# Sums of the seven products' weights made in DRAM, and the other half of the tokens normalized first

## The chip, the cores and the metric

The kernel runs on one core of a Trainium2 chip. TensorE (PE) multiplies matrices, its weights loaded by a unit of its own (PEld); VectorE (DVE) and ScalarE (ACT) work on whole tiles; GpSimd (POOL) does little here but issue transfers; SyncE (SP) issues the others. All transfers run on the core's 16 DMA engines, POOL's through the queue that the profile calls software_dynamic, SP's through hardware_dynamic. The metric is the device time of one execution in microseconds.

## What is computed

Two layers of a hybrid block over 512 latent tokens and 256 context tokens with 1024 channels. Each layer normalizes, runs three mixers side by side (convolution, attention, retention), merges them through gates and an output projection, and then a gated feed-forward part. For layer 0 it runs on all 768 tokens, and it is what the change is about:

```python
def conv_ffn(h, w_up, dw_w, dw_b, w_down):
    gt, val = jnp.split(h @ w_up, 2, axis=-1)
    gt = dwconv(gt, dw_w, dw_b)
    return (jax.nn.silu(gt) * val) @ w_down
...
        y = merge_branches(gates, a, att, ret, w_pa[l], w_pb[l], w_pc[l]) @ w_out[l]
        x = x + g1 * y
...
        x = x + g2 * conv_ffn(modulate(rms_norm(x, norm2_g[l]), sh2, sc2),
                              w_up[l], ffn_dw_w[l], ffn_dw_b[l], w_down[l])
        if not last:
            xc = xc + cg2 * conv_ffn(modulate(rms_norm(xc, norm2_g[l]), csh2, csc2),
                                     w_up[l], ffn_dw_w[l], ffn_dw_b[l], w_down[l])
```

`modulate` uses one shift and scale for the latent tokens and others for the context.

## The kernel before

Activations stand with channels in partitions and tokens along the row, in tiles of 128 channels x 768 tokens, latent tokens (0 to 511) ahead of the context (512 to 767). A product in fp32 is made of three matmuls: weight and token operand are each split into a high and a low part (hi is ACT's copy in a rounded format, lo is DVE's difference), and hi x hi, hi x lo and lo x hi are added up in PSUM.

**Weights.** A stream of tiles (class `Stream`) of 128x1024 fp32, 512 KB each, is loaded by SP from `wstream` into buffers `raw`. `prepare` splits them some tiles ahead of use: ACT at L224 (whi), DVE at L225 (wlo), into a rotating set of slots that come free when PE has used the tile in them.

**Seven products.** `up_seven` in `ffn` makes w_up's product for layer 0, in 22 chunks of 128 columns. Weights and tokens are cut in two by two blocks (channels 0 to 511 and 512 to 1023; gate and value columns; first and second half of the tokens, 384 each), and seven products take the place of eight. Of the weights these need the blocks 11, 12 and 22 as they are and S1 = 21 + 22, S2 = 11 + S1, S3 = 11 + 21, S4 = 12 + S2. `operand` makes the four sums per chunk with four additions on DVE (L188) in the raw tiles, and ACT and DVE split each operand by itself (tiles wop, 128x512). Of the tokens, `split_tokens` makes the operands in two goes: after tokens 0 to 383 are normalized, those of 11 and 12; after tokens 384 to 767, those of S2, S1, S3, 22 and S4, in that order. A go normalizes blocks b (DVE L691, ACT L693) of 384 tokens; the second half crosses token 512, so its blocks are made in pieces of 128 and 256. t2 and t3 are the sums (L716, L717, L722, L730), hh and hl their split parts. PE goes through the products in `up_order`: 11 and 12 of chunks 0 to 2, then S2 of all three (`s2_first`, both halves of its four channel blocks in turn), S1, S3, and so on. `product` (L1693) is the line of all their matmuls.

**Before that stage**, `last_chunks` makes w_out's last four output chunks half by half (`parts`), so that the first half of the tokens can be normalized while the second is multiplied.

**Mixers.** Layer 0 runs the steps of the string `ORDER[0]` one after the other ('K Q0 R0 Q1 A R1 G0 C G1 G2 G3 P0 ...'): dense products of the step, with attention and retention run beside them in pieces. On POOL's queue in that stage stand `attsp<-att` (an attention result, 384 KB, written to DRAM from a tile in a shared set of slots, four times), `ij<-ij` (a table that retention's decay factors kdec and dec are made of) and, from 470 us, rowa.

**Residual updates.** After every four chunks a down phase multiplies by w_down; its results dx are added to xup in DRAM by accumulating transfers (POOL, `accum_op`), 32 in all.

A scheduler orders each engine's instructions; within an engine they run in that order, and a transfer is issued by its engine in its turn, after what it waits for.

Of the kernel before, what the change touches and what calls it, by code (L numbers as in the profile page):

```python
# [25 lines left out]
P = 128  # L26
# [23 lines left out]
ATTR, RETR, CONVR, ADAR = (1.0, 1.0), (1.4, 1.6), (0.4, 0.4), (0.06, 0.28, 0.4, 0.33)  # L50
QLAG = 2
# [64 lines left out]
def up_blocks(c, row, half):  # L116

    return [(("w_up", 0, (4 * half + j) * P, row * DFF + c * P), P) for j in range(4)]
# [10 lines left out]
class Stream:  # L129
# [3 lines left out]
    def __init__(self, k, dram):  # L133
        self.k, self.dram = k, dram


        self.items, self.units, self.need, self.blocks = [], [0], [], []
        self.ab, self.de = {}, {}

        def load():  # L140
            self.blocks.append([])
            return len(self.blocks) - 1

        def tiles(n):
            for _ in range(n):
                self.items.append(load())
                self.units.append(self.units[-1] + 2)
                self.need.append(len(self.blocks))
        tiles(NUP)
        for x in up_order():  # L150
# [16 lines left out]
        self.raw, self.s1 = {}, {}  # L167
# [6 lines left out]
        self.tag = 0  # L174

    def issue(self, upto):
        while self.issued < min(upto, self.need[self.limit - 1]):
            i = self.issued
            t = self.k.raw_pool.tile([P, SUB], F32, tag="raw", name=f"raw{i}")
            self.k.nc.sync.dma_start(t, self.dram[i])  # L180
            self.raw[i] = t
            self.issued += 1

    def operand(self, name, c):

        nc = self.k.nc
# [12 lines left out]
        if name == "S2":  # L199
            self.s1[c] = self.k.S("s1")[:, :Q]  # L200
            add(self.s1[c], d, e)
            add(e, a, e)
            add(a, self.s1[c], a)
            return a
        return self.s1.pop(c) if name == "S1" else e

    def prepare(self, base):
# [3 lines left out]
        while self.done < self.limit and self.units[self.done + 1] - self.units[base] <= 2 * WB:  # L211
# [42 lines left out]
    def next_operand(self, *x):  # L254
        self.step()
        self.off = SUB
        assert self.items[self.cur] == x
        return self.split[self.cur]
# [29 lines left out]
class Kern:  # L288
# [32 lines left out]
    def mm(self, out, w, x, start, stop):  # L321
        return self.nc.tensor.matmul(out, w, x, start=start, stop=stop)  # L322
# [58 lines left out]
    def last_chunks(self, key, xs, segs, hold, evac, norm, lead=0, limit=None):  # L381
# [23 lines left out]
        halves = parts(segs)  # L405
# [211 lines left out]

    def rstd2(self, pts, name, y=None):
# [55 lines left out]
    def split_tokens(self, l, xs, ops):  # L674
# [19 lines left out]

        def parts(name, t, i):
            ops.setdefault(name, [None, None])[i] = self.split(t, TALL, "h")

        def gen(segs):
# [3 lines left out]
            if not half:  # L702
# [783 lines left out]
    def run(self):  # L1486
        nc, io = self.nc, self.io
        self.ada_blocks = []
        self.sq2 = self.crow = None
        self.setup()  # L1490
# [35 lines left out]
    def layer_mixers(self, l, last, segs, T, xs, xsp, first, h2):  # L1526
# [38 lines left out]
        for step in ORDER[l].split():  # L1565
# [48 lines left out]
        def evac(m, pts):  # L1614
            for pt, o, c in kinds(pts):
# [7 lines left out]
                                None if l else NUP + 2 * UPFIRST)  # L1623

    def ffn(self, l, h2, xs, segs, T, gen, xsp, xup):
# [57 lines left out]
        def up_seven():  # L1683
# [12 lines left out]
            one, two = slice(0, HALF), slice(HALF, TALL)  # L1696
# [260 lines left out]
```

## Time and profile before

| | |
|---|---|
| time, median of 3 runs | 2299.3 us (2297.7 to 2299.55) |
| profiled execution, its own time | 2294.79 us |
| its span | 2293.0 us |
| PE busy | 2226.6 us, 97% |
| DVE busy | 1665.9 us, 73% |
| ACT busy | 998.2 us, 44% |
| POOL busy | 104.3 us, 5% |
| DMA, mean | 106 GB/s; q1 (SP) 169.03 MB, q0 (POOL) 72.36 MB |

The profile is of one execution. Busy time is an engine's own; the lists of waits name the engine that waited, its tile and line, and after the arrow what released it. Times of single instructions are from the start of the span. The seven-product stage runs from about 815 to 1290 us, layer 0's mixers from about 100 to 600.

### The profile page before, as it was taken

The numbers are of one execution on the slowest core, as the hardware profiler recorded it, in microseconds if no ns is written. First come the engines' busy times: TensorE is split into PE (matmuls) and PEld (weight loads), VectorE is DVE, ScalarE is ACT, GpSimd is POOL, SyncE is SP. The second block draws the span as 40 slices with busy tenths as digits, with TensorE's granted clock in tenths as the row PEclk, the third lists the DMA queues.
The fourth block names the chain that finished last, engine by engine and source line by source line (L and its number), as shares of the span: only waits on it lengthen the run. The fifth ranks groups of instructions, "written<-read, shape, count | busy, mean of one in ns | idle before, by whom it ended". The sixth has DMA issues, their size and how long they took to land.

```text
span 2293.0 us, 34300 instructions
## 1 busy us (share of the span) xinstructions
PE 2226.6 (97%) x13386; PEld 2033.7 (89%) x13386; DVE 1665.9 (73%) x3384; ACT 998.2 (44%) x1784; POOL 104.3 (5%) x177
## 2 busy tenths in 40 slices
PE   6999999999999979999999999999999999999998
PEld 4988999999999969999999889888887889888887
DVE  6877959799885488676676769878799656744445
ACT  3465653332332256455454444665443334423333
POOL 0000000000010000100101100000001100000000
PEclk9999999999999989999999999999999999999999
DMA  8211111123343202544635412111126623422221
GB/s 316 100 68 54 45 56 46 38 92 138 121 165 120 77 36 109 138 113 118 156 96 144 182 74 75 51 51 61 56 87 236 236 93 106 170 101 94 100 92 37
DMA packets 70961, 243.57 MB, mean 106 GB/s; under 512 B 8496, under 2 KB 10816, under 8 KB 70800
## 3 DMA queue, kind: packets, MB, share of 16 engines
q1 hardware_dynamic: 50400, 169.03, 20.9%
q0 software_dynamic: 20400, 72.36, 11.0%
q8 instruction: 105, 1.72, 0.3%
q14 instruction: 56, 0.46, 0.1%
HBM read 218.82 MB, written 22.54 MB: 105 GB/s over the span
## 4 chain that ended last, share of the span: by engine, by line
PE 85%; DVE 6%; issue 5%; ACT 2%; DMA 2%; POOL 0%; SPq 0%; DVEq 0%; POOLq 0%; ACTq 0%
PE pd L322 57%; PE ps L322 14%; PE pd L1693 10%; PE ps L1693 2%; PE ps L1350 2%; DVE wlo L225 1%; PE ps L1263 0%; ACT whi L224 0%; DMA x<-xt 0%; DMA rowa<-wadt 0%; DMA xup<-dx 0%; DVE cacc L799 0%; DMA raw<-wstream 0%; DVE fy L1742 0%; DVE qq L1298 0%
## 5 line engine op out<-in xcount | busy, mean ns | idle before, releaser
L224 ACT ACTIVATE whi<-raw 128x1024 fp32r<-128x1024 f32 x236 | 249.7, 1060 | 637.2 <-PE pd L322 496.0
L322 PE MATMUL pd<-hh,whi 128*128 128x384 f32 (+2 forms) x1472 | 470.5, 359 | 0.0
L322 PE MATMUL pd<-hh,wlo 128*128 128x384 f32 (+2 forms) x1472 | 470.4, 359 | 0.0
L322 PE MATMUL pd<-hl,whi 128*128 128x384 f32 (+2 forms) x1472 | 469.7, 359 | 0.0
L225 DVE TENSOR_TENSOR wlo<-raw,whi 128x1024 fp32r<-128x1024 f32 x236 | 288.1, 1222 | 180.3 <-ACT whi L224 176.5
L322 PEld LDWEIGHTS pd<-hh,whi 128*128 128x128 f32 x1472 | 270.6, 188 | 28.2 <-issue 1.7
L322 PEld LDWEIGHTS pd<-hh,wlo 128*128 128x128 f32 x1472 | 271.5, 188 | 25.8 <-issue 1.1
L322 PEld LDWEIGHTS pd<-hl,whi 128*128 128x128 f32 x1472 | 270.9, 188 | 25.6 <-issue 0.7
L1693 PE MATMUL pd<-hh,wop 128*128 128x384 f32 x1024 | 267.5, 337 | 18.9 <-ACT wop L224 16.4
L799 DVE SCALAR_TENSOR_TENSOR cacc<-u,vec,cacc 128x497 f32<-128x497 f32 (+9 forms) x360 | 221.0, 650 | 2.0
L1693 PEld LDWEIGHTS pd<-hh,wop 128*128 128x128 f32 x1024 | 186.6, 189 | 21.3 <-ACT wop L224 16.7
L1693 PE MATMUL pd<-hl,wop 128*128 128x384 f32 x512 | 172.3, 337 | 0.0
L1333 ACT ACTIVATE prob<-ps,amx,qrs 128x256 f32<-128x256 f32 (+1 forms) x144 | 93.8, 656 | 90.4 <-DVE amx L1328 75.2
L322 PE MATMUL pd<-whi,hl 128*128 128x256 f32 x416 | 118.9, 287 | 5.5 <-DVE hl L756 5.5
L322 PE MATMUL pd<-whi,hh 128*128 128x256 f32 x416 | 119.3, 289 | 1.7 <-ACT hh L753 1.7
L322 PE MATMUL pd<-wlo,hh 128*128 128x256 f32 x416 | 117.9, 284 | 0.0
L224 ACT ACTIVATE wop<-raw 128x512 fp32r<-128x512 f32 x132 | 81.1, 627 | 65.4 <-DVE raw L188 24.5
L322 PE MATMUL pd<-hidh,whi 128*128 128x512 f32 (+1 forms) x302 | 104.4, 358 | 2.8 <-DVE x L1783 2.8
L225 DVE TENSOR_TENSOR wop<-raw,wop 128x512 fp32r<-128x512 f32 x132 | 87.7, 687 | 25.0 <-ACT wop L224 24.4
L322 PE MATMUL pd<-hidl,whi 128*128 128x512 f32 (+1 forms) x302 | 103.5, 355 | 0.0
L322 PE MATMUL pd<-hidh,wlo 128*128 128x512 f32 (+1 forms) x302 | 103.3, 355 | 0.0
L601 DVE SCALAR_TENSOR_TENSOR rowa<-rowa,crow 128x768 f32<-128x768 f32 (+1 forms) x144 | 94.4, 686 | 4.0 <-DMA rowa<-wadt 4.0
(299 smaller groups left out, 4279.5 us busy)
## 6 DMA issues: line engine op xcount, KB each, us to landing
raw<-wstream SPq DMA_DIRECT2D x280, 512.0 KB, 3.5
rowa<-wadt POOLq DMA_DIRECT2D x72, 512.0 KB, 4.5
xup<-dx POOLq DMA_DIRECT2D x32, 384.0 KB, 5.9
adar<-wada SPq DMA_DIRECT2D x16, 384.0 KB, 7.6
rawa<-wada SPq DMA_DIRECT2D x8, 512.0 KB, 4.2
x<-xt SPq DMA_DIRECT2D x8, 384.0 KB, 7.7
crow<-crow POOLq DMA_DIRECT2D x8, 384.0 KB, 4.3
x<-xt POOLq DMA_DIRECT2D x8, 384.0 KB, 4.4
```

Source lines behind the costliest of these rows:

```text
L224: nc.scalar.activation(hi, r, AF.Copy)
L225: nc.vector.tensor_tensor(lo, r, hi.bitcast(F32), op=ALU.subtract)
L322: return self.nc.tensor.matmul(out, w, x, start=start, stop=stop)
L601: nc.vector.scalar_tensor_tensor(out, raw[:, a:b], 1.0, t[:, o:o + b - a], op0=ALU.mult, op1=ALU.mult, accum_out=acc[:, c, j, h:h + 1])
L799: nc.vector.scalar_tensor_tensor(acc[:, a:b], u[:, a + d:b + d], w(k), acc[:, a:b], op0=ALU.mult, op1=ALU.add)
L1333: nc.scalar.activation(pr[:, o - k0:o - k0 + c], pt[:, :c], AF.Exp, scale=rs, bias=mx[:, 2:3], accum_out=sm[:, j:j + 1])
L1350: nc.tensor.transpose(pt[:, b * P:b * P + P], pr[:, o + b * P:o + b * P + P], self.ident)
L1693: nc.tensor.matmul(pt, w[:, b], x, start=start and k == 0 and i == 0, stop=k == 3 and i == 2, skip_group_check=not start)
```

## The change

The weights of the blocks 11, 12, 21 and 22 come as inputs of their own (`wup0` to `wup23`), for six batches of four chunks, the last of two; they are no longer in `wstream`. `make_sums` is called after the steps named in `SUMAT` and makes S1, S3, S2 and S4 of a batch in DRAM: a copy of one block, then a transfer that adds another to it (S2 adds S1, S4 adds S2), all issued by POOL. The first copies of a batch wait for the last matmul that was written down before the call. In `Stream` the operands go in pairs: a raw tile is filled by two loads of 256 KB, from the blocks or from the sums, and split whole, 128x1024, at one line with the other weights; `operand` and its DVE additions are gone. `last_chunks` takes the halves in the other order where the seven products follow, `split_tokens` makes 11 and 12 of tokens 384 to 767 and the rest after tokens 0 to 383, and `one` and `two` change places with that. Of the second go, all sums and splits that are not S2's are ordered behind S2's last split on DVE.

```diff
@@ -48,6 +48,7 @@
          'K Q0 Q1 R0 A G0 C R1 G1 G2 G3 P0 P1 P2 P3 T T T T T T')
 ATT_LEAD, RET_LEAD = (3, 2), (1, 1)
 ATTR, RETR, CONVR, ADAR = (1.0, 1.0), (1.4, 1.6), (0.4, 0.4), (0.06, 0.28, 0.4, 0.33)
+SUMAT = ("R1", "G1", "G2", "G3", "P1", "P2")
 QLAG = 2
 HOLDO, HOLDD = (4, 4), (4, 6)
 LEADO, LEADD, LEADB = 2, 2, ((0, 0, 0), (4, 0, 4))
@@ -113,9 +114,26 @@
...
-def up_blocks(c, row, half):
-    return [(("w_up", 0, (4 * half + j) * P, row * DFF + c * P), P) for j in range(4)]
+BATCH = 4
+BLOCKS = ("11", "12", "21", "22")
+SUMS = (("S1", "21", ("22",)), ("S3", "11", ("21",)), ("S2", "11", ("S1",)), ("S4", "12", ("S2",)))
+def batches():
+    return [range(c, min(c + BATCH, NFF)) for c in range(0, NFF, BATCH)]
@@ -152,57 +171,38 @@
...
-            name, c = x
-            if name == "11":
-                self.ab[c] = load()
-                self.blocks[-1] = up_blocks(c, 0, 0) + up_blocks(c, 0, 1)
-            elif name == "S2":
-                self.de[c] = load()
-                self.blocks[-1] = up_blocks(c, 1, 1) + up_blocks(c, 1, 0)
-            self.items.append(x)
-            self.units.append(self.units[-1] + 1)
-            self.need.append(len(self.blocks))
-        tiles(DEPTH * NSUB - len(self.blocks))
+            if n % 2 == 0:
+                tiles(1)
+                self.blocks[-1] = None
+                self.ops[self.items[-1]] = []
+            self.ops[self.items[-1]].append(x)
+            self.place[x] = (len(self.items) - 1, Q * (n % 2))
+            n += 1
+        tiles(DEPTH * NSUB - 8 * NFF // 4 - sum(x is not None for x in self.blocks))
...
-            self.k.nc.sync.dma_start(t, self.dram[i])
+            if i in self.ops:
+                for j, x in enumerate(self.ops[i]):
+                    self.k.nc.sync.dma_start(t[:, j * Q:j * Q + Q], self.k.up_operand(*x))
+            else:
+                self.k.nc.sync.dma_start(t, self.dram[self.row(i)])
...
-    def operand(self, name, c):
-        nc = self.k.nc
-        a, b = (self.raw[self.ab[c]][:, o:o + Q] for o in (0, Q))
-        add = lambda out, x, y: nc.vector.tensor_tensor(out, x, y, op=ALU.add)
-        if name == "11":
-            return a
-        if name == "12":
-            return b
-        if name == "S4":
-            add(b, a, b)
-            return b
-        d, e = (self.raw[self.de[c]][:, o:o + Q] for o in (0, Q))
-        if name == "22":
-            return d
-        if name == "S2":
-            self.s1[c] = self.k.S("s1")[:, :Q]
-            add(self.s1[c], d, e)
-            add(e, a, e)
-            add(a, self.s1[c], a)
-            return a
-        return self.s1.pop(c) if name == "S1" else e
@@ -212,15 +212,9 @@
             i = self.done
             x = self.items[i]
             self.issue(self.need[i])
-            if isinstance(x, tuple):
-                r = self.operand(*x)
-                t = pool.tile([P, SUB], F32R, tag=("whi", "wlo")[self.tag], name=f"wop{i}")
-                self.tag = 1 - self.tag
-                hi, lo = t[:, :Q], t[:, Q:]
-            else:
-                r = self.raw.pop(x)
-                hi = pool.tile([P, SUB], F32R, tag="whi", name=f"whi{i}")
-                lo = pool.tile([P, SUB], F32R, tag="wlo", name=f"wlo{i}")
+            r = self.raw.pop(x)
+            hi = pool.tile([P, SUB], F32R, tag="whi", name=f"whi{i}")
+            lo = pool.tile([P, SUB], F32R, tag="wlo", name=f"wlo{i}")
             nc.scalar.activation(hi, r, AF.Copy)
             nc.vector.tensor_tensor(lo, r, hi.bitcast(F32), op=ALU.subtract)
             self.split[i] = (hi, lo)
@@ -319,7 +316,8 @@
         return self.small.tile([P, cols], F32, tag=tag, name=self.nm(tag))
     def mm(self, out, w, x, start, stop):
-        return self.nc.tensor.matmul(out, w, x, start=start, stop=stop)
+        self.last_mm = self.nc.tensor.matmul(out, w, x, start=start, stop=stop)
+        return self.last_mm
     @contextmanager
@@ -402,7 +400,7 @@
                     tiles.append(self.W.cur)
         tiles.append(self.W.cur + (self.W.off == SUB))
         gen = None
-        halves = parts(segs)
+        halves = parts(segs)[::-1] if limit else parts(segs)
         for i, hs in enumerate(halves):
             for j, m in enumerate(range(KC - hold, KC)):
                 evac(m, self.dense(None, xs, hs, ws[j]))
@@ -615,6 +613,25 @@
...
+    def up_operand(self, name, c):
+        b, j = divmod(c, BATCH)
+        t = self.up_sums[b][name] if name in self.up_sums[b] else self.io[f"wup{4 * b + BLOCKS.index(name)}"]
+        return t[:, j * Q:j * Q + Q]
+    def make_sums(self, b):
+        n = len(batches()[b]) * Q
+        src = {x: self.io[f"wup{4 * b + i}"] for i, x in enumerate(BLOCKS)}
+        for name, base, more in SUMS:
+            t = src[name] = self.up_sums[b][name] = self.dram.tile([P, n], F32, name=f"sum{name}_{b}")
+            first = self.nc.gpsimd.dma_start(t, src[base], max_dma_last_dim=2048)
+            info = mybir.DependencyInfo(mybir.DependencyClass.Sync, mybir.DependencyReason.DATA)
+            self.tc.add_manual_dep(first.ins, self.last_mm.ins.name, info, reason="later")
+            for x in more:
+                self.nc.gpsimd.dma_start(t, src[x], accum_op=ALU.add, max_dma_last_dim=2048)
@@ -692,14 +709,25 @@
...
+        done = []
         def parts(name, t, i):
-            ops.setdefault(name, [None, None])[i] = self.split(t, TALL, "h")
+            hi, lo = ops.setdefault(name, [None, None])[i] = self.S("hh", F32R), self.S("hl", F32R)
+            nc.scalar.activation(hi, t, AF.Copy)
+            op = nc.vector.tensor_tensor(lo, t, hi.bitcast(F32), op=ALU.subtract)
+            (done.append if name == "S2" else later)(op)
+        def later(op):
+            if done:
+                info = mybir.DependencyInfo(mybir.DependencyClass.NoSync, mybir.DependencyReason.DATA)
+                self.tc.add_manual_dep(op.ins, done[-1].ins.name, info, reason="order")
         def gen(segs):
             half = segs[0][0]
             self.sq_rstd(segs, r)
             yield
-            if not half:
+            if half:
@@ -719,7 +747,7 @@
             yield "S2"
             for i in range(2):
                 u, b = raw["u", i], raw["11", i]
-                nc.vector.tensor_tensor(u, b, u, op=ALU.subtract)
+                later(nc.vector.tensor_tensor(u, b, u, op=ALU.subtract))
                 parts("S1", u, i)
             yield "S1"
             for i in range(2):
@@ -727,7 +755,7 @@
             yield "S3"
             for i in range(2):
                 b = raw["12", i]
-                nc.vector.scalar_tensor_tensor(t2[i], t2[i], -1.0, b, op0=ALU.mult, op1=ALU.subtract)
+                later(nc.vector.scalar_tensor_tensor(t2[i], t2[i], -1.0, b, op0=ALU.mult, op1=ALU.subtract))
                 parts("22", t2[i], i)
             yield "22"
             for i in range(2):
@@ -1582,6 +1611,8 @@
                 self.ret_in[i] = self.ret_inputs(i, segs, T)
             elif kind == "T":
                 ths.append(self.gate(2, len(ths), segs))
+            if l == 0 and step in SUMAT:
+                self.make_sums(SUMAT.index(step))
         self.finish(mix)
         if l == 0:
             self.finish(ada)
@@ -1620,7 +1651,7 @@
         norm = self.norm(l, 1, xs, h2) if last else self.split_tokens(l, xs, h2)
         return self.last_chunks(lambda m, k: ("w_out", l, k * P, m * P), mm, even(segs), HOLDO[l], evac, norm, LEADO,
-                                None if l else NUP + 2 * UPFIRST)
+                                None if l else NUP + UPFIRST)
     def ffn(self, l, h2, xs, segs, T, gen, xsp, xup):
         nc = self.nc
@@ -1693,7 +1724,7 @@
                         nc.tensor.matmul(pt, w[:, b], x, start=start and k == 0 and i == 0, stop=k == 3 and i == 2,
                                          skip_group_check=not start)
-            one, two = slice(0, HALF), slice(HALF, TALL)
+            one, two = slice(HALF, TALL), slice(0, HALF)
             def p11(c):
                 X[c], g[c], val[c] = self.dps()[:, :HALF], self.S("fg"), self.S("fv")
```

On POOL, in the mixers' stretch around the third and fourth attention step, there stood before:

```order
L1469 DMA attsp1_103<-att_375_2472 128x768
L1469 DMA attsp2_104<-att_483_3043 128x768
L1554 DMA ij_646_3940<-ij 128x514
L1469 DMA attsp3_105<-att_590_3664 128x768
L590 DMA rowa0_2_0_5548<-wadt 128x1024
```

and now, from the last sum of batch 2 on (the sums' names end in the batch, counted from 0; L627 are plain copies, L632 accumulating ones):

```order
L632 DMA sumS4_2_3101<-sumS2_2_3098 512x512
L632 DMA sumS1_3_3433<-wup15 512x512
L627 DMA sumS3_3_3436<-wup12 512x512
L627 DMA sumS2_3_3439<-wup12 512x512
L632 DMA sumS3_3_3436<-wup14 512x512
L632 DMA sumS2_3_3439<-sumS1_3_3433 512x512
L627 DMA sumS4_3_3442<-wup13 512x512
L1497 DMA attsp2_104<-att_483_3067 128x768
L632 DMA sumS4_3_3442<-sumS2_3_3439 512x512
L1583 DMA ij_646_3988<-ij 128x514
L1497 DMA attsp3_105<-att_590_3712 128x768
```

The transfers attsp2, ij and attsp3, which stood one behind the other, now stand behind and between those of batches 2 and 3.

On ACT, in the last attention step before retention, there stood (prob and probt are the attention weights, kdec retention's factors; the semaphores that each waits for are in brackets):

```order
L1333 ACTIVATE prob_636_3886,asm_635_3883<-ps_633_3879,amx_634_3882,qrs_118_830 128x256 [waits DVE_49,Activation_49]
L1351 ACTIVATE probt_637_3890<-ps_638_3891 128x256 [waits PE_49]
L1365 ACTIVATE att_590_3664<-ps_639_3895 128x128 [waits PE_49]
L1351 ACTIVATE probt_640_3917<-ps_641_3918 128x256 [waits PE_49]
L1351 ACTIVATE probt_642_3922<-ps_643_3923 128x256 [waits PE_49]
```

and now:

```order
L1361 ACTIVATE prob_636_3934,asm_635_3931<-ps_633_3927,amx_634_3930,qrs_118_830 128x256 [waits DVE_49,Activation_49]
L1379 ACTIVATE probt_637_3938<-ps_638_3939 128x256 [waits DMASW5_49,PE_49]
L1393 ACTIVATE att_590_3712<-ps_639_3943 128x128 [waits PE_49]
L1379 ACTIVATE probt_640_3965<-ps_641_3966 128x256 [waits PE_49]
L1379 ACTIVATE probt_642_3970<-ps_643_3971 128x256 [waits PE_49]
```

The order is the same; probt_637 now has the slot of the tile that attsp2 reads, and waits for that transfer's landing (DMASW5).

On DVE, at the start of the seven-product stage, from the last pieces of the second go on, there stood:

```order
L691 SCALAR_TENSOR_TENSOR b_1103_8429<-x_963_6899,coef0_86,rstd_1039_7736 128x256
L730 SCALAR_TENSOR_TENSOR t2_1099_8413<-t2_1099_8413,b_1072_8205 128x768
L716 TENSOR_TENSOR t3_1104_8438<-b_1103_8429,b_1102_8420 128x768
L717 SCALAR_TENSOR_TENSOR t2_1105_8439<-t3_1104_8438,b_1069_8196 128x768
L722 TENSOR_TENSOR b_1102_8420<-b_1069_8196,b_1102_8420 128x768
L451 TENSOR_TENSOR hl_1107_8443<-t2_1105_8439,hh_1106_8442 128x768
L188 TENSOR_TENSOR s1_1108_8448<-raw77_8446 128x512
L188 TENSOR_TENSOR s1_1109_8459<-raw78_8455 128x512
L188 TENSOR_TENSOR raw77_8446<-raw74_7928,raw77_8446 128x512
L188 TENSOR_TENSOR raw78_8455<-raw75_7988,raw78_8455 128x512
```

and now, from the pair splits that stand among the second go's first part on:

```order
L219 TENSOR_TENSOR wlo79_8536<-raw79_8525,whi79_8535 128x1024
L744 TENSOR_TENSOR t3_1098_8489<-b_1097_8484,b_1096_8479 128x768
L219 TENSOR_TENSOR wlo80_8543<-raw80_8532,whi80_8542 128x1024
L745 SCALAR_TENSOR_TENSOR t2_1099_8490<-t3_1098_8489,b_1064_8227 128x768
L717 TENSOR_TENSOR hl_1101_8494<-t2_1099_8490,hh_1100_8493 128x768
L708 SCALAR_TENSOR_TENSOR b_1102_8497<-x_958_6961,coef0_86,rstd_1039_7808 128x384
L708 SCALAR_TENSOR_TENSOR b_1102_8497<-x_959_6963,coef0_86,rstd_1039_7808 128x384
L708 SCALAR_TENSOR_TENSOR b_1103_8502<-x_962_6969,coef0_86,rstd_1039_7808 128x384
L708 SCALAR_TENSOR_TENSOR b_1103_8502<-x_963_6971,coef0_86,rstd_1039_7808 128x384
L744 TENSOR_TENSOR t3_1104_8507<-b_1103_8502,b_1102_8497 128x768
L745 SCALAR_TENSOR_TENSOR t2_1105_8508<-t3_1104_8507,b_1069_8273 128x768
L717 TENSOR_TENSOR hl_1107_8512<-t2_1105_8508,hh_1106_8511 128x768
```

The blocks are made in one piece, the additions of L188 are gone, L722 and L730 (now L750 and L758) follow behind hl_1107, and the pair splits wlo78 to wlo80 stand ahead of S2's first split.

## Rows read from the trace of the kernel before

**Rows 1.** Head of the page: busy us (share of the span) xinstructions.

```profile
PE 2226.6 (97%) x13386; PEld 2033.7 (89%) x13386; DVE 1665.9 (73%) x3384; ACT 998.2 (44%) x1784; POOL 104.3 (5%) x177
```

**Rows 2.** Waits of PE: line <- released by: us in total, times, longest us.

```profile
PE pd L1693 <- ACT wop L224: 16.4, 1, 16.4
...
PE ps L322 <- ACT dx L1774: 2.7, 5, 1.1
```

**Rows 3.** Timeline of PE, 820 to 870: start us, us, instruction [idle before <-releaser].

```profile
828.16 0.34 PE L1693 MATMUL ps<-hh,wop 128*128 128x384 f32 x1
844.90 0.69 PE L1693 MATMUL pd<-hh,wop 128*128 128x384 f32 x1 [16.41 <-ACT wop L224]
```

**Rows 4.** Timeline of DVE, 817 to 845.

```profile
817.54 1.14 DVE L691 SCALAR_TENSOR_TENSOR b<-x,coef,rstd 128x384 f32<-128x384 f32 x2
...
833.86 2.72 DVE L691 SCALAR_TENSOR_TENSOR b<-x,coef,rstd 128x128 f32<-128x128 f32 x8
...
840.22 0.96 DVE L451 TENSOR_TENSOR hl<-t,hh 128x768 fp32r<-128x768 f32 x1
841.10 1.28 DVE L188 TENSOR_TENSOR s<-raw 128x512 f32<-128x512 f32 x2
```

**Rows 5.** Windows: us, busy us (xinstructions) of PE, PEld, DVE, ACT, POOL, PEclk, DMA share, GB/s.

```profile
845.00:851.00 6.00, 5.87 (x18) 5.36 (x19) 6.00 (x11) 4.33 (x8) 0.00 (x0) 0.51 0.00 0
851.00:861.00 10.00, 10.00 (x59) 10.00 (x58) 8.77 (x13) 6.59 (x12) 0.00 (x0) 1.00 0.30 100
...
1000.00:1050.00 50.00, 50.00 (x290) 50.00 (x289) 34.25 (x67) 24.82 (x47) 9.09 (x12) 1.00 0.69 166
...
300.00:350.00 50.00, 49.81 (x399) 45.52 (x396) 29.74 (x70) 21.18 (x56) 1.08 (x2) 1.00 0.13 46
```

**Rows 6.** Page, costliest groups: xcount | busy, mean ns | idle before.

```profile
L225 DVE TENSOR_TENSOR wlo<-raw,whi 128x1024 fp32r<-128x1024 f32 x236 | 288.1, 1222 | 180.3 <-ACT whi L224 176.5
```

**Rows 7.** Timeline of POOL, 190 to 400 and 1000 to 1060.

```profile
292.51 0.54 POOL L1469 DMA_DIRECT2D attsp<-att  x1 [42.25 <-ACT att L1365]
318.06 0.54 POOL L1554 DMA_DIRECT2D ij<-ij  x1 [25.00 <-DVE u L773]
...
1017.91 0.85 POOL L1775 DMA_DIRECT2D xup<-dx  x1 [10.07 <-ACT dx L1774]
```

**Rows 8.** Timeline of ACT, 208 to 226 and 318 to 336.

```profile
212.09 0.78 ACT L1333 ACTIVATE prob<-ps,amx,qrs 128x512 f32<-128x512 f32 x1 [1.61 <-issue]
...
322.26 0.39 ACT L1351 ACTIVATE probt<-ps 128x256 f32<-128x256 f32 x1
...
325.18 0.48 ACT L888 ACTIVATE kdec<-lg,ij 128x8 f32<-128x8 f32 x2
```

**Rows 9.** Timeline of PE, 318 to 336.

```profile
333.25 1.16 PE L322 MATMUL ps<-rv,kf 128*128 128x128 f32 x8
```

**Rows 10.** Transfers, 150 to 340: queue: packets, MB, share; issues: xcount, KB, landing us.

```profile
q1 hardware_dynamic: 2304, 8.39, 12.5%
...
attsp<-att POOLq DMA_DIRECT2D x4, 384.0 KB, 2.9
```

**Rows 11.** The tile dx, written to xup by 32 adding transfers.

```profile
DMA to landing us min/median/max: 4.5/5.9/8.4
```

**Rows 12.** Transfers, 1200 to 1235: queue share, and the issues on it.

```profile
q0 software_dynamic: 1584, 4.72, 71.2%
...
xup<-dx POOLq DMA_DIRECT2D x8, 384.0 KB, 5.5
rowa<-wadt POOLq DMA_DIRECT2D x3, 512.0 KB, 5.7
```

**Rows 13.** Timeline of PE: the matmuls that release batches 1, 2 and 3.

```profile
227.58 0.28 PE L322 MATMUL ps<-kl,qq 128*128 128x256 f32 x1
...
258.75 0.52 PE L322 MATMUL ps<-kl,qq 128*128 128x512 f32 x2
...
281.33 0.28 PE L322 MATMUL ps<-kl,qq 128*128 128x256 f32 x1
```

More of the change, by code (lines that the diff above doesn't have):

```diff
@@ L113, in up_order, with up_weights @@
     return out + [("22", NFF - 1), ("S4", NFF - 1)]
-def up_blocks(c, row, half):
-    return [(("w_up", 0, (4 * half + j) * P, row * DFF + c * P), P) for j in range(4)]
+BATCH = 4
[3 more added lines that the diff above has]
+    return [range(c, min(c + BATCH, NFF)) for c in range(0, NFF, BATCH)]
+def up_weights(w):
+    out = []
+    for cs in batches():
+        for row in range(2):
+            for half in range(2):
+                out.append(np.concatenate([w[(4 * half + j) * P:(4 * half + j + 1) * P,
+                                             row * DFF + c * P:row * DFF + c * P + P] for c in cs for j in range(4)], 1))
+    return out
 def parts(segs):
@@ L137, in __init__ @@
         self.items, self.units, self.need, self.blocks = [], [0], [], []
-        self.ab, self.de = {}, {}
+        self.ops, self.place = {}, {}
+        n = 0
         def load():
@@ L154, in __init__ @@
                 continue
-            name, c = x
-            if name == "11":
-                self.ab[c] = load()
-                self.blocks[-1] = up_blocks(c, 0, 0) + up_blocks(c, 0, 1)
-            elif name == "S2":
-                self.de[c] = load()
-                self.blocks[-1] = up_blocks(c, 1, 1) + up_blocks(c, 1, 0)
-            self.items.append(x)
-            self.units.append(self.units[-1] + 1)
-            self.need.append(len(self.blocks))
-        tiles(DEPTH * NSUB - len(self.blocks))
+            if n % 2 == 0:
[6 more added lines that the diff above has]
+        tiles(DEPTH * NSUB - 8 * NFF // 4 - sum(x is not None for x in self.blocks))
         self.limit = self.total = len(self.items)
-        self.raw, self.s1 = {}, {}
+        self.raw = {}
         self.split = {}
@@ L173, in __init__ @@
         self.kept = None
-        self.tag = 0
     def issue(self, upto):
@@ L179, in issue, with row @@
             t = self.k.raw_pool.tile([P, SUB], F32, tag="raw", name=f"raw{i}")
-            self.k.nc.sync.dma_start(t, self.dram[i])
+            if i in self.ops:
[3 more added lines that the diff above has]
+                self.k.nc.sync.dma_start(t, self.dram[self.row(i)])
             self.raw[i] = t
             self.issued += 1
-    def operand(self, name, c):
-        nc = self.k.nc
-        a, b = (self.raw[self.ab[c]][:, o:o + Q] for o in (0, Q))
-        add = lambda out, x, y: nc.vector.tensor_tensor(out, x, y, op=ALU.add)
-        if name == "11":
-            return a
-        if name == "12":
-            return b
-        if name == "S4":
-            add(b, a, b)
-            return b
-        d, e = (self.raw[self.de[c]][:, o:o + Q] for o in (0, Q))
-        if name == "22":
-            return d
-        if name == "S2":
-            self.s1[c] = self.k.S("s1")[:, :Q]
-            add(self.s1[c], d, e)
-            add(e, a, e)
-            add(a, self.s1[c], a)
-            return a
-        return self.s1.pop(c) if name == "S1" else e
+    def row(self, i):
+        return i - sum(j < i for j in self.ops)
     def prepare(self, base):
@@ L254, in next_operand @@
     def next_operand(self, *x):
[L255 to L258, printed above, removed]
+        i, o = self.place[x]
+        if i > self.cur:
+            self.step()
+            self.off = SUB
+        assert self.cur == i
+        hi, lo = self.split[i]
+        return hi[:, o:o + Q], lo[:, o:o + Q]
 class Side:
@@ L1489, in run @@
         self.sq2 = self.crow = None
+        self.up_sums = [{} for _ in batches()]
         self.setup()
@@ L1939 @@
     shapes = {k: v.shape for k, v in arrays.items()}
-    shapes["wstream"] = (DEPTH * NSUB, P, SUB)
+    for i, w in enumerate(up_weights(a["w_up"][0])):
+        arrays[f"wup{i}"] = w
+        shapes[f"wup{i}"] = w.shape
+    shapes["wstream"] = (DEPTH * NSUB - 2 * NFF, P, SUB)
     shapes["wada"] = (NADA, P, SUB)
@@ L1947 @@
         k.run()
-    arrays["wstream"] = _blocks(k.W.blocks, a)
+    arrays["wstream"] = _blocks([x for x in k.W.blocks if x is not None], a)
     wada = np.zeros((NADA, P, SUB), np.float32)
```

## The prediction

> **What bounds the kernel now.** I read the head of the page first: TensorE (PE) is busy for 97% of the span [rows 1]. With PE that full, an edit is worth only what it takes out of PE's idle time, or puts into it. The list of what PE waited for comes second: the longest wait is 16.4 us, once, at the product of the seven-product stage (L1693), for a weight operand split on ScalarE (ACT, L224) [rows 2]. Third, the stretch of that wait, engine by engine. PE starts the last of the six products that need only the first half of the tokens at 828.16 and S2 at 844.90 [rows 3]. VectorE (DVE) is at work nearly all that time: normalization of the second half in pieces of 128 and 256 columns, the token sums, the last split of tokens at 840.22, ending at 841.18, and then weight sums (L188) from 841.10 on, six of them before PE can start [rows 4]; ACT splits the finished operand and PE begins. So one chain holds PE: tokens, then weight sums. Fourth, the windows: after the wait the granted clock is 0.51 (the 1.2 GHz level) from 845 to 851, where 18 matmuls take 6 us, and 1.00 in the next ten, with 59. In the body of the stage, 1000 to 1050, PE is busy 50.00 of 50 us and DVE 34: DVE's sums hold up nothing there. Where the new transfers go, in the mixers, PE has no room either: 49.81 of 50 from 300 to 350 [rows 5].
>
> **What the change gives in the seven-product stage.** The weight sums leave DVE: 88 adds of 0.64 us, 56 us of busy time. All but the six in the wait lie beside a full PE and are worth nothing. In the wait I count along DVE up to the end of S2's last split, 841.18 before. The sum that S2 doesn't need (L730) and two of L722 go behind that split, 3 x 0.95 = 2.9 us less. Eight blocks become one piece of 384 columns where they were two (two whole ones took 1.14 us, eight pieces 2.72, so a block 0.57 for 0.68 [rows 4]), 0.9 us less. Three pair splits of weights now stand among them, 1.22 us each [rows 6], 3.7 us more. The first half, now the one in pieces, is about 1.3 us later by the same prices. That is 841.18 + 1.2, some 842.4 for S2's second part, and no sums after it, where PE waited until 844.90. Moreover PE works on S2's first part ahead of that, from about 836, when that part's tokens are split. S2 is 36 matmuls. Before, 18 ran at the low clock and 18 at the full one, 0.17 us each, to 854.0. Now the second 18 start at 842.4 and end at 845.5 at the full clock or 848.4 at the low one. The gain is 5.6 to 8.5 us; I take 7, as a part of the low-clock stretch now lies where PE would wait anyway, and 4 to 8 as range, for at the later products PE then stands closer behind DVE.
>
> Two smaller terms. 33 more tiles of 512 KB are loaded, in halves, but in a window with a DMA share of 0.69 PE lost nothing [rows 5]: 0, at most 3. And in the first down phase the tiles of the residual updates have one slot fewer ahead, so that ACT waits for earlier landings; PE lost 2.7 us to that tile before [rows 2]: I put down 1, between 0 and 3.
>
> **What it costs in the mixers.** Six batches are queued on GpSimd (POOL): four plain copies and four accumulating transfers each, of 1 MB (512 KB in the last batch). A batch's sums wait on POOL for its copies and for one another, so whatever stands behind them there waits too. Behind batch 3 stand attsp2, ij and attsp3, which were issued when their data were ready, 292.51 and 318.06 for the first two [rows 7]. Who waits for them: with the change ACT's copy at 322.26 writes a buffer that attsp2 still reads, and PE's products right behind read that copy; ACT's kdec at 325.18 reads ij [rows 8], and PE needs what comes of it at 333.25 [rows 9].
>
> The price of a copy: SP's queue moved 8.39 MB in the mixers with 12.5% of the 16 engines' 190 us, 2.83 us per MB; a transfer of 1 MB (1.049 million bytes) takes the engines 3.0 us [rows 10]. No row shows a copy from DRAM to DRAM. An accumulating transfer: the nearest is xup<-dx, 384 KB, with 5.9 us to landing [rows 11], while attsp, a plain one of that size, has 2.9 [rows 10]: twice, so 6.0 us per MB. The bounds: not less than a plain one, 3.0; and by its own queue's share, 71.2% of 35 us less three plain loads (1.57 MB, 4.5 us), eight took 20.4 us [rows 12], 6.8 per MB. I take 6.0, as that stretch is busier than the mixers, and let the loads' share there count for nothing.
>
> Now the queue. PE releases batch 1 at 227.9, batch 2 at 259.3 and batch 3 at 281.6 [rows 13]. From 227.9 until attsp2 has landed the engines owe three batches but for the last sum: 12 copies x 3.0 = 36, 11 sums x 6.0 = 66, and 1.1 each for attsp1 and attsp2: 104 us. With 3 us of issue, landing and gaps that is 335.1. Both later releases come while the batch ahead is still in the queue, so they don't matter. ACT wanted the buffer at 322.26: it stands for 12.9 us, and PE with it, whose order is fixed. ij is issued behind the last sum and lands near 343.6, where kdec would come at 338.1; from kdec to PE's need there were 8 us, so that I put down 0.5. After a wait as long as that PE starts at the low clock: after the 16.4 us it lost 18 x (0.33 - 0.17) = 2.9 us to that [rows 5], so 3. attsp0 lands at about 206 by this count and is wanted at 212.09 [rows 8]. Batches 4 and 5 have 60 us before the next transfer that stands behind them.
>
> **Sum**, against the profiled execution of 2294.8 us: -7 + 12.9 + 0.5 + 3 + 1 = +10.4, so 2305.2. The median of the runs shown is 4.5 above that execution: 2310.
>
> **Rivals.** (a) *The sums land in time*, and only the gain is left. The turning point: 227.9 + 3 + 36 + 2.2 + 11p = 322.3 gives p = 4.8 us for an accumulating transfer of 1 MB. For it speaks that a part of the 5.9 us is waiting behind other transfers; against it that the fastest xup<-dx took 4.5 [rows 11], and that of attsp's 2.9 us only 1.1 are movement: 4.5 less the 1.8 that don't move, and less 0.3 of longer issue, is 2.4 us for 0.393 MB, 6.4 for 1 MB. Time: 2294.8 - 7 + 1 + 4.5 = 2293, with the gain's range 2291 to 2296. The Trainium skill (DMA: Bandwidth & Descriptors, Anatomy of one DMA) has one line for every transfer of this queue, 2.0 us plus the bytes over 436e3 per us, with no surcharge for adding: an estimate from that page is 4.4 us for 1 MB, 2.4 of it movement, and by that rule the queue would be through some 45 us earlier and this rival would hold. By the landings of xup<-dx and attsp, 5.9 against 2.9, the trace disagrees for transfers that add.
>
> (b) *The two cancel.* With p between 4.8 and 5.4 ACT waits up to 6 us, PE loses less to the clock, and the time is 2296 to 2304: no change.
>
> (c) *The issue is dearer too.* A batch's transfers are cut into 512 rows of 2 KB, where those of the trace have 128; a plain issue took POOL 0.55 us, an adding one 0.85 [rows 7]. If these grow with the rows, to 2.1 and 3.5, the chain on POOL lengthens and attsp2 lands at 351, a wait of 29 us: 2326. The Trainium skill (the same section) says that many descriptors can be emitted before their cost shows. No row here has such a count; by that sentence this rival falls.
>
> (d) *The reversal doesn't bring PE forward.* The pair splits of S2's weights wait for slots of the last w_out tiles and stand in front of the token sums; if S2's tokens come at 845 for it, the gain is 2, and with the wait in the mixers the time is 2315.
>
> **How the numbers follow.** The forecast (attsp2 late by 7 to 20 us) 0.38; (a) 0.26; (b) 0.14; (c), or a price near 6.8, 0.16; (d) 0.06. A measurement of this kernel can tell about 0.2%, 4.6 us, from no change: faster is below 2294.7, slower above 2303.9. Faster: (a) and a sliver of (b), 0.27. Same: 0.14. Slower: the rest, 0.59. The range goes from (a)'s end to (c): 2291 to 2328; outside lie (c) together with a dear sum, and a gain of over 8.
>
> **What would show it.** In the profile after: PE waits in the attention's products near 322 to 335 for ACT's copy, and ACT for the landing of attsp; the queue of POOL is busy without gaps from 228 to 345, where a sum of 1 MB lands 7 to 9 us after its issue when alone; the granted clock is about 0.5 for some us after that wait; S2 starts near 836 of before's time, with no wait of more than some 8 us left there. The forecast is wrong if the attention's stretch shows no wait (then (a)), if POOL's issues themselves take microseconds (then (c)), or if the load of half a tile ends a wait of PE in the seven-product stage.

## The result, and the profile after

The changed kernel takes 2317.9 us (median of 4 runs, 2315.45 to 2318.89) where the kernel before takes 2298.5 in the same comparison: a ratio of 1.0084 with the interval 1.0067 to 1.0102. It is slower by 19.4 us; 2310 was forecast, between 2291 and 2328.

The list of what PE waited for in the changed kernel (line <- released by: us in total, times, longest us) has a new head:

```profile
PE ps L319 <- ACT probt L1379: 23.9, 1, 23.9
PE ps L319 <- DVE sq L661: 14.7, 1, 14.7
PE pd L1724 <- ACT hh L716: 9.1, 3, 6.7
...
PE ps L319 <- DVE kb L981: 5.5, 7, 3.5
...
PE ps L319 <- ACT dx L1805: 0.6, 3, 0.2
```

The 16.4 us of the seven-product stage [rows 2] are gone; what is left there is 9.1 in three pieces. In their place stand 23.9 us at the attention, and one of 3.5 at kb. The timelines of ACT and PE show where (start us, us, instruction, idle before it and what ended that):

```profile
216.20 0.78 ACT L1361 ACTIVATE prob<-ps,amx,qrs 128x512 f32<-128x512 f32 x1 [2.52 <-DMA attsp<-att]
...
326.27 0.21 ACT L1361 ACTIVATION_READ_ACCUMULATOR prob<-ps,amx,qrs 128x1 f32 x1
351.35 0.38 ACT L1379 ACTIVATE probt<-ps 128x256 f32<-128x256 f32 x1 [24.87 <-DMA attsp<-att]
...
361.00 0.49 ACT L916 ACTIVATE kdec<-lg,ij 128x8 f32<-128x8 f32 x2 [6.91 <-DMA ij<-ij]
```

```profile
217.12 0.44 PE L1378 MATMUL ps<-cst,prob 128*128 128x128 f32 x2 [0.71 <-ACT prob L1361]
...
327.23 0.66 PE L1378 MATMUL ps<-cst,prob 128*128 128x128 f32 x4
351.79 1.98 PE L319 MATMUL ps<-probt,vt 128*64 128x128 f32 x16 [23.90 <-ACT probt L1379]
...
364.90 1.59 PE L319 MATMUL ps<-rq,rk 64*128 64x128 f32 x8 [3.45 <-DVE kb L981]
```

The long wait is at the instruction that the prediction named: ACT's copy, at 322.26 before [rows 8], stands for the landing of attsp2, and kdec after it for ij. A short one, at 216, stands for attsp0. Why attsp2 was late, POOL's timeline tells:

```profile
271.65 1.44 POOL L632 DMA_DIRECT2D sumS<-sumS  x1 [11.48 <-DMA sumS<-sumS]
272.75 1.61 POOL L627 DMA_DIRECT2D sumS<-wup  x2
...
317.18 1.03 POOL L632 DMA_DIRECT2D sumS<-wup  x1 [1.14 <-DMA sumS<-wup]
317.82 1.67 POOL L627 DMA_DIRECT2D sumS<-wup  x2
334.25 1.04 POOL L632 DMA_DIRECT2D sumS<-wup  x1 [14.76 <-DMA sumS<-wup]
336.46 1.03 POOL L632 DMA_DIRECT2D sumS<-sumS  x1 [1.17 <-DMA sumS<-wup]
337.11 1.03 POOL L627 DMA_DIRECT2D sumS<-wup  x1
337.75 0.96 POOL L1497 DMA_DIRECT2D attsp<-att  x1
350.84 1.07 POOL L632 DMA_DIRECT2D sumS<-sumS  x1 [12.13 <-issue]
351.50 0.99 POOL L1583 DMA_DIRECT2D ij<-ij  x1
```

attsp2 was issued at 337.75, 45 us later than before [rows 7], in a row of sums in which most issues waited for the landing of one ahead. The transfers from 228 to 352 (queue: packets, MB, share of 16 engines; then issues with median us to landing):

```profile
q0 software_dynamic: 9232, 24.91, 82.8%
q1 hardware_dynamic: 1008, 3.67, 8.5%
...
sumS<-sumS POOLq DMA_DIRECT2D x6, 1024.0 KB, 10.2
...
attsp<-att POOLq DMA_DIRECT2D x2, 384.0 KB, 13.3
ij<-ij POOLq DMA_DIRECT2D x1, 257.0 KB, 9.5
```

The seven-product stage, and the start of the last down phase, in PE's timeline:

```profile
862.17 0.34 PE L1724 MATMUL ps<-hh,wlo 128*128 128x384 f32 x1
869.16 1.33 PE L1724 MATMUL pd<-hh,whi 128*128 128x384 f32 x3 [6.66 <-ACT hh L716]
...
875.78 0.80 PE L1724 MATMUL pd<-hh,whi 128*128 128x384 f32 x3 [1.15 <-ACT hh L716]
...
1337.14 0.78 PE L319 MATMUL pd<-hidh,whi 128*128 128x512 f32 x2 [3.99 <-DVE x L1814]
```

**Where the time went.** One and the same matmul can be followed through both traces. The release of batch 3, 281.33 before [rows 13], is at 285.42: 4.1 us later. Of these, 3.0 came in the first 60 us, ahead of the first transfer of a sum (issued at 168.17), and aren't the change's: two experiments below (e7 and e10), whose code is the same there as before, had 3.2 and 4.4 at 828 (it is before's profiled execution that was short, 2294.8 against a median of 2298.5). The other 1.1 came at 217, where ACT waited for attsp0. The last of the first six products, 828.16 before [rows 3], is at 862.17: 34.0 later, so the mixers cost 31. They are the 1.1 at attsp0, the two waits, 23.9 and 3.5, and the low clock after each of the two (columns as in [rows 5]; the granted clock is the third from the end):

```profile
351.80:354.80 3.00, 3.00 (x19) 2.67 (x20) 0.00 (x0) 1.21 (x5) 1.11 (x3) 0.50 0.64 85
...
364.90:368.20 3.30, 3.30 (x16) 3.02 (x17) 2.18 (x5) 0.22 (x1) 0.00 (x0) 0.53 0.00 0
```

There PE's matmuls fall from 28.1 us behind those of before to 29.3, and from 32.7 to 34.1: 1.2 and 1.4. By the end of the stage, where PE's wait before the last down phase begins at 1333.15 for 1309.63 before, 23.5 are left: the stage gave 10.5. Without the 3.0 of the start 31 - 10.5 = 20.5; the medians differ by 19.4.

### The profile page after: what moved, and what is told of

Read it like the earlier page. It is cut to its first block, busy times and chain, and to the rows that moved or that the text cites. A ratio compares the mean times of both kernels' runs of the same rounds, so it can differ in the third digit from the quotient of the medians.

```text
span 2316.6 us, 34409 instructions
## 1 busy us (share of the span) xinstructions
PE 2232.2 (96%) x13386; PEld 2037.1 (88%) x13386; DVE 1604.8 (69%) x3219; ACT 989.0 (43%) x1707; POOL 144.5 (6%) x225
## 3 DMA queue, kind: packets, MB, share of 16 engines
q1 hardware_dynamic: 66240, 186.34, 23.5%
q8 instruction: 105, 1.72, 0.3%
## 4 chain that ended last, share of the span: by engine, by line
PE 53%; issue 3%; DVE 3%; DMA 1%; ACT 1%; POOL 0%; DVEq 0%; POOLq 0%; ACTq 0%
PE pd L319 31%; PE pd L1724 11%; PE ps L319 8%; PE ps L1724 2%; PE ps L1378 1%; DVE wlo L219 1%; DMA crow<-crow 0%; DMA rowa<-wadt 0%; ACT whi L218 0%; DVE cacc L827 0%; DMA rl<-attsp 0%; DVE qq L1326 0%; ACT dx L1805 0%; DMA raw<-wstream 0%; DVE rowa L599 0%
## 5 line engine op out<-in xcount | busy, mean ns | idle before, releaser
L218 ACT ACTIVATE whi<-raw 128x1024 fp32r<-128x1024 f32 x313 | 331.4, 1061 | 748.0 <-PE pd L319 492.0
L219 DVE TENSOR_TENSOR wlo<-raw,whi 128x1024 fp32r<-128x1024 f32 x313 | 382.3, 1222 | 258.8 <-ACT whi L218 245.1
L319 PEld LDWEIGHTS pd<-hh,whi 128*128 128x128 f32 x1472 | 270.9, 188 | 28.0 <-issue 1.8
L1724 PE MATMUL pd<-hh,whi 128*128 128x384 f32 x512 | 171.8, 339 | 9.1 <-ACT hh L716 9.1
L1724 PE MATMUL pd<-hl,whi 128*128 128x384 f32 x512 | 172.3, 336 | 0.5 <-DVE hl L717 0.4
L1724 PE MATMUL pd<-hh,wlo 128*128 128x384 f32 x512 | 171.7, 336 | 0.0
L1724 PEld LDWEIGHTS pd<-hh,whi 128*128 128x128 f32 x512 | 96.5, 189 | 12.0 <-ACT hh L716 10.1
L588 POOL DMA_DIRECT2D rowa<-wadt x72 | 39.1, 543 | 950.1 <-DVE wlo L219 737.1
```

Source lines behind the costliest of these rows:

```text
L218: nc.scalar.activation(hi, r, AF.Copy)
L219: nc.vector.tensor_tensor(lo, r, hi.bitcast(F32), op=ALU.subtract)
L319: self.last_mm = self.nc.tensor.matmul(out, w, x, start=start, stop=stop)
L588: nc.gpsimd.dma_start(loaded[-1], self.io["wadt"][l, 8 * pc + c])
L1724: nc.tensor.matmul(pt, w[:, b], x, start=start and k == 0 and i == 0, stop=k == 3 and i == 2, skip_group_check=not start)
```

## The experiments

All times are given against runs of the kernel before made beside them on the same chip: medians 2295.0 (e1 to e4), 2294.7 (e5 to e8) and 2295.1 (e9, e10).

**e1: no transfers for the sums.**

```diff
-            if l == 0 and step in SUMAT:
-                self.make_sums(SUMAT.index(step))
...
-        t = self.up_sums[b][name] if name in self.up_sums[b] else self.io[f"wup{4 * b + BLOCKS.index(name)}"]
+        name = {"S1": "21", "S2": "11", "S3": "11", "S4": "12"}.get(name, name)
+        t = self.io[f"wup{4 * b + BLOCKS.index(name)}"]
```

> The changed kernel without the sums' transfers: the operands S1 to S4 are loaded from plain blocks, so that the products are of other weights than they should be; every engine's order and every load stays. Theory (the 23.9 us wait of PE in the attention and what follows from it is the price of the sums; the gain in the seven-product stage is separate): no wait at the attention, 2318 - 24 - 3.5 - 2.8 = 2288, the stage's gain of 10 to 11 us against before unchanged. Rival (the loss is from something else that the change moved in the mixers, slots or order): the wait stays in part and the time is over 2300.

2287.5 us, ratio 0.9956 (0.9940 to 0.9973), 7.5 us below before. No wait of the attention is left among PE's:

```profile
PE ps L319 <- DVE sq L662: 15.3, 1, 15.3
PE pd L1723 <- ACT hh L717: 8.6, 3, 6.7
PE pd L319 <- DVE hl L785: 4.8, 3, 2.3
```

So what the mixers lost is the sums' doing, and the rest of the change gains 7.5 us by the medians, 10 by the ratio, whose interval is 6 to 14 us.

**e2: one batch fewer ahead of attsp2.**

```diff
-SUMAT = ("R1", "G1", "G2", "G3", "P1", "P2")
+SUMAT = ("R1", "G1", "G2", "P1", "P2", "P3")
```

> The changed kernel with batches 3 to 5 released after P1, P2, P3 in place of G3, P1, P2, so that one batch fewer stands ahead of attsp2 and ij; every engine's own order but POOL's stays. Theory (attsp2 and ij wait for their turn in POOL's queue): with one batch of 1 MB transfers less, some 35 us of queue, attsp2 lands near 316 to 322, PE waits 0 to 2 us, and the time is 2288 to 2292. Rival (the traffic itself slows the mixers, wherever it lies): the wait or its like comes back later, at P1 to P3, and the time stays over 2300.

2295.9 us, ratio 1.0001 (0.9989 to 1.0014): between the two expectations. The wait of 23.9 became one of 6.2, for the same transfer and earlier:

```profile
313.26 0.28 ACT L1393 ACTIVATE att<-ps 128x128 f32<-128x128 f32 x1 [0.37 <-PE ps L319]
323.81 0.56 ACT L1361 ACTIVATE prob<-ps,amx,qrs 128x256 f32<-128x256 f32 x1 [10.27 <-DMA attsp<-att]
```

attsp2 landed at 323.8 where 316 to 322 was expected; but with the instructions in the same order the tiles had got other slots, and ACT now wanted attsp2's at 313.5 and not near 326. Nothing came back at P1 to P3. The queue is right as the cause; when a slot is wanted is not a thing that stays when transfers move.

**e3: spills and ij issued by ACT, batches where they were.**

```diff
-        self.nc.gpsimd.dma_start(dst[:, :w], t[:, :w])
+        self.nc.scalar.dma_start(dst[:, :w], t[:, :w])
...
-            nc.gpsimd.dma_start(self.ij[:, :4 * P + 2], io["ij"])
+            nc.scalar.dma_start(self.ij[:, :4 * P + 2], io["ij"])
```

> The changed kernel with the spills of attention and retention and the table ij issued by ACT in place of POOL, batches where they were. Theory (the place in POOL's queue is the cause): attsp2 is issued near 297 and lands within 6 us although the engines are 90% busy with sums, ij is there near 330, PE waits under 2 us, and the time is 2287 to 2293. Rival (the 16 DMA engines are so full that any transfer lands late, whoever issues it): attsp2 lands after 320 here too and the time is 2305 or more.

2291.6 us, ratio 0.9990 (0.9978 to 1.0002). The sums' queue is as full as in the changed kernel, and yet (transfers from 228 to 345):

```profile
q0 software_dynamic: 8596, 22.68, 82.8%
...
attsp<-att ACTq DMA_DIRECT2D x3, 384.0 KB, 6.9
ij<-ij ACTq DMA_DIRECT2D x1, 257.0 KB, 8.1
```

attsp lands in 6.9 us where it took 13.3 behind the sums after an issue 45 us late, and PE's wait of 23.9 is gone. What remains is ij: issued on ACT at 327.5, after ACT's copies there, it took 8.1 us among the sums where 3.0 was usual, and PE waited 3.7 us in retention. So it is the place in POOL's queue that made attsp2 late, and full engines add some us to a transfer of any queue.

**e4: rows of 8 KB in place of 2 KB.**

```diff
-max_dma_last_dim=2048
+max_dma_last_dim=8192
```

> The changed kernel with the batches' transfers cut into 128 rows of 8 KB in place of 512 of 2 KB. Theory (a sum's price is by bytes, about 6 us of the engines for 1 MB): an issue takes 0.55 and 0.85 us where it took 0.65 and 1.05, but attsp2 still lands 20 us or more late and the time is 2311 to 2318. Rival (a good part of the price is per row): a sum takes a third less of the engines, attsp2 lands under 12 us late, and the time is 2304 or less.

2313.4 us, ratio 1.0078 (1.0062 to 1.0093). The wait at the attention is 16.9 us for 23.9; POOL's issues in the timeline mostly take 0.83 for an adding transfer where they took 1.03 to 1.07. In the 117 us from 228 to 345 the queue moved 25.18 MB with a share of 82.6%, 96.6 us of the engines; with short rows it was 24.91 MB with 102.7. By the MB that is 3.84 us of the engines for 4.12: a quarter of the rows takes 7% off the price, so most of it goes by bytes. attsp2 kept ACT waiting for 17.9 us, a little under the 20 expected.

**e5: a stretch without batches.** Issue by ACT as in e3, and

```diff
-SUMAT = ("R1", "G1", "G2", "G3", "P1", "P2")
+SUMAT = ("R1", "G0", "G1", "P1", "P2", "P3")
```

> The changed kernel with the spills and ij issued by ACT and the batches released after R1, G0, G1, P1, P2, P3, so that no batch is in flight from about 295 to 355, where attsp2, ij and attsp3 are issued. Theory (queue place and shared engines make up the whole loss): no wait over 1 us at the attention or retention, and the time is that of the kernel without sums, 7 to 9 us below before. Rival (the traffic costs something wherever it is): 3 us below before or less.

2287.5 us, ratio 0.9961 (0.9948 to 0.9973), 7.2 us below before. The sums are made, all of them, and cost nothing that shows:

```profile
PE ps L319 <- DVE sq L661: 14.8, 1, 14.8
PE pd L1724 <- ACT hh L716: 8.8, 3, 6.7
PE pd L319 <- DVE hl L784: 4.8, 3, 2.3
```

This version beats both kernels.

**e6: as e5, the halves in the old order.**

```diff
-        halves = parts(segs)[::-1] if limit else parts(segs)
+        halves = parts(segs)
...
-            if half:
+            if not half:
...
-            one, two = slice(HALF, TALL), slice(0, HALF)
+            one, two = slice(0, HALF), slice(HALF, TALL)
```

> As e5, but with the halves in the old order: tokens 0 to 383 first, S2's blocks in pieces of 128 and 256 again; sums from DRAM and the ordering of the other splits stay. Theory (the weight sums that left DVE, and PE starting on S2's first part, make the gain; the halves' order is worth the pieces on the path, under 1.5 us): 5.5 to 9 us below before. Rival (the halves' order makes half the gain): 2 to 4 us below before.

2286.3 us, ratio 0.9961 (0.9949 to 0.9974): the same as e5. PE's wait for S2 is 6.47 us where it was 6.66. The order of the halves is worth nothing that shows.

**e7: the halves alone,** in the kernel before: e6's three edits the other way round.

> The kernel before with the halves reversed and nothing else: sums on DVE as before, no transfers. Theory: DVE's chain is 0.9 us shorter in S2's blocks and begins 1.3 us later, and the six sums stay in front of PE: within 1.5 us of before. Rival (the halves' order makes half the gain): 3 to 5 us below before.

2292.9 us, ratio 0.9991 (0.9982 to 1.0001). The wait is 14.83 us for 16.41:

```profile
831.40 0.34 PE L1693 MATMUL ps<-hh,wop 128*128 128x384 f32 x1
846.57 0.69 PE L1693 MATMUL pd<-hh,wop 128*128 128x384 f32 x1 [14.83 <-ACT wop L224]
```

That is 1.6 us in the wait, and in the time no difference that can be told from none.

**e8: e5's batches, spills and ij in POOL's queue.**

> As e5, but with spills and ij in POOL's queue: attsp1 stands behind 12 copies and 10 sums that are released from 165 on, so by the 119 us that as many took in the changed kernel it lands near 285, where ACT wants its buffer at 273. Theory (the count of what stands ahead sets the landing): PE waits 10 to 15 us near 275 and nothing near 322 to 352; the time is 6 to 10 us above before. Rival (what was late was special to attsp2, ij and retention): no wait at 275, and the time is that of e5.

2305.4 us, ratio 1.0039 (1.0025 to 1.0052), 10.6 above before. The wait moved to attsp1, as the count had it:

```profile
269.52 0.29 ACT L1393 ACTIVATE att<-ps 128x128 f32<-128x128 f32 x1
286.20 0.56 ACT L1361 ACTIVATE prob<-ps,amx,qrs 128x256 f32<-128x256 f32 x1 [16.39 <-DMA attsp<-att]
```

It landed at 286.2, 285 was expected, and PE waited 14.7 us; from 322 to 352 PE waits for nothing longer than 0.4. The time is a little above the 6 to 10 us expected. A transfer is late by what stands ahead of it in the queue, whichever it is.

**e9: e6 without the ordering of the later sums and splits** (in `later`, `if done:` became `if False:`).

> As e6 (spills and ij by ACT, early batches, halves in the old order), but without the ordering of the other sums and splits behind S2's: L722 twice and L730 stand in front of S2's second split again, 2.9 us of DVE. Theory (each us on DVE's chain in front of S2 is a us of PE): PE waits 2 to 3 us longer at S2, 4 to 6 us below before. Rival (PE has S2's first part to work on and doesn't feel it): as e6, 7 to 9 us below before.

2286.9 us, ratio 0.9962 (0.9948 to 0.9975): as e6; PE's wait for S2 is 6.47 us in both. The 2.9 us that were to be felt aren't there.

**e10: that ordering alone, in the kernel before** (the same `parts` and `later`, the sums still on DVE).

> The kernel before with that ordering alone: the two L722 and L730 stand behind S2's second split, the six weight sums on DVE follow that split as before. Theory: the sums begin 2.9 us earlier, PE's 16.4 us become 13 to 14, a part is given back at S1, whose tokens come later: 1 to 3 us below before. Rival (what follows S2 is late by as much): within 1 us of before.

2297.3 us, ratio 1.0010 (1.0001 to 1.0019): 2 us above before, where 1 to 3 below or less than 1 either way was expected. PE's wait is 16.30 us for 16.41. DVE's timeline shows why:

```profile
835.54 0.96 DVE L728 SCALAR_TENSOR_TENSOR t<-t,b 128x768 f32<-128x768 f32 x1
837.41 0.96 DVE L700 TENSOR_TENSOR hl<-t,hh 128x768 fp32r<-128x768 f32 x1 [0.91 <-ACT hh L699]
838.28 2.72 DVE L691 SCALAR_TENSOR_TENSOR b<-x,coef,rstd 128x128 f32<-128x128 f32 x8
841.67 0.96 DVE L727 TENSOR_TENSOR t<-b,b 128x768 f32<-128x768 f32 x1 [0.67 <-ACT b L693]
842.66 0.96 DVE L728 SCALAR_TENSOR_TENSOR t<-t,b 128x768 f32<-128x768 f32 x1
844.53 0.96 DVE L700 TENSOR_TENSOR hl<-t,hh 128x768 fp32r<-128x768 f32 x1 [0.91 <-ACT hh L699]
845.41 1.29 DVE L188 TENSOR_TENSOR s<-raw 128x512 f32<-128x512 f32 x2
```

Where L722 and L730 had stood, DVE now waits 0.91, 0.67 and 0.91 us for ACT. From the start of the eight pieces to the last split it is 6.25 us here and was 833.86 to 840.22, 6.36, before [rows 4]. The chain goes from DVE to ACT and back; those three sums had filled its gaps.

## Why the prediction was right, and where it was not

**The mechanism and the sign were right:** attsp2 behind batch 3, ACT's copy for its slot, PE behind ACT; then ij and kdec; then the low clock. e1 shows that the sums cost all of it, e3 that it is POOL's queue, and e8 moves the wait to attsp1 by the same count.

**The size was luck in part.** The forecast proper was attsp2 late by 7 to 20 us, and ACT waited 24.9. In the traces the mixers cost 31 us for the 16.4 of the sum, and the stage gave 10.5 for 6, so that two errors partly cancelled. The time lies well within the range because that had been drawn out to the price of rival (c), whose dearer issues didn't come.

**The term that was mis-sized is attsp2's landing.** It was put at 335.1, 12.9 us late, and came at 351.4. With the 4.1 us taken off by which the kernel was behind there already, that is 12 later than forecast; in PE it made 23.9 for 12.9. The prices weren't at fault. From 168 to 174.5 two copies move and nothing else:

```profile
q0 software_dynamic: 436, 1.72, 78.7%
```

That is 5.1 us of the engines for 1.72 MB, 3.1 for a copy of 1 MB, for which 3.0 was taken. Of the 102.7 us that the queue took from the engines between 228 and 352, 12 copies of 3.1 and two spills of 1.1 leave 63 for some 11 sums, 5.7 each, for which 6.0 was taken. Two things were mis-sized in the sum. SP's loads had 8.5% of the same engines, 10.5 us, and were put at nothing. And the engines weren't always busy: from batch 1's release, here at 232, to the landing the DMA share is 0.95,

```profile
232.00:351.40 119.40, 95.79 (x736) 87.07 (x734) 72.74 (x189) 59.37 (x160) 21.60 (x26) 0.91 0.95 240
```

which leaves 6 us idle, where 3 were allowed. Together that is 13.5 us more than forecast, and the queue's own work was some 1.5 less than the 104 taken: 12. This is an account from the shares; no run takes SP's loads away. The same count put attsp0's landing at 206, with 6 us to spare; it came at 216.2, 213.2 without the late start, and cost PE the 1.1 us that the sum hadn't.

**ij** was put at 0.5 us and cost 3.5. It landed 9.5 us after its issue, at 361.0, and kept ACT waiting for 6.9 us, where 5.5 follow from the forecast. And the 8 us from kdec to PE's need had been taken as free: 3.9 of them are the work on ACT and DVE between kdec, at 361.00, and PE's start at 364.90. **The clock's 3 us** came as a sum, 2.6, but by luck: 1.2 after the wait for attsp2, for which all 3 had been put down, and 1.4 after the one at kb, for which none had.

**The gain of 7 us held as a sum**: 7.5 in e1, 7.2 in e5, 8.5 in e6 and 8.2 in e9 by the medians (by the ratios 9 to 10, with intervals from 6 to 14). In the traces it is larger up to the end of the stage, 10.5 for the changed kernel, in part because the first down phase's waits for dx fell to 0.6 where a loss of 1 was put down; the wait at the last down phase, 3.99 us for 2.85, takes some of it back. Its steps held less well. S2's first part came at 869.16 and its second at 875.78, which is 835.2 and 841.8 in before's time, for 836 and 842.4: right. But the two edits from which the shorter chain was worked out give nothing alone (e7: 1.6 us in the wait, e10: none), and the gain is there without either (e6 for the halves, e9 for both; e9 has neither the new halves nor the ordering). What e9 keeps is the sums in DRAM, with the pairs in which they are then loaded and split, which no run takes apart. So the gain is the weight sums' leaving, as far as the runs tell: PE no longer needs the six of them after the last token split, and it can begin on S2's first part. The step that failed was to add up instructions along DVE as if DVE were never waiting there: pieces, L722 and L730 lay in its gaps, the pair splits in part too, it seems, and the errors cancelled.

**The rivals.** (a), that the sums land in time, would have needed 4.8 us for a sum, and (b), that the two cancel, one between 4.8 and 5.4; 5.7 was the price, near the 6.0 worked out from xup<-dx. (c), dearer issues: a plain issue of 512 rows took POOL 0.64 to 1.08 us (0.64 where nothing was issued just ahead) and an adding one 1.04 in the median, at most 1.44, not 2.1 and 3.5, so this rival fell. The Trainium skill (DMA: Bandwidth & Descriptors, Anatomy of one DMA) says that many descriptors can be emitted before their cost shows: there the trace agrees, with 0.1 to 0.2 us for four times the rows. (d), S2's tokens only at 845, didn't happen: 841.8.

## What to carry to other kernels

Before a long chain of transfers is put on an engine's queue, list what stands behind it there until the chain is through, and when the landing of each is wanted; a transfer that was early by 27 us can be the one that stops TensorE. Count all that shares the DMA engines, and the gaps of the chain, not the chain's bytes alone; or issue the small urgent transfers from another engine and keep the long chain out of the stretch in which they are wanted. A sum of instruction times along one engine is the length of a path only where that engine doesn't wait within it.

## What the runs showed of the hardware that was not expected

Adding 1 MB to 1 MB in DRAM takes the 16 DMA engines 5.7 us, nearly twice the 3.1 of a copy, and with 128 rows in place of 512 the queue of both takes 7% less (e4). POOL's issue of such a transfer grows little with the rows: 1.04 us in the median for 512 rows, 0.83 for 128. And while one queue holds 83% of the engines, a transfer of 384 KB issued on another queue lands in 6.9 us (e3), where it took 13.3 in the full queue and 2.9 in the kernel before [rows 10].
